# Four of eight K-pairs by seven products, and feature-major products sorted by length

## The chip, the cores and the metric

The kernel runs on one core of one Trainium2 chip. The metric is the device time of one execution in microseconds. Three runs of the kernel before took 2154.32, 2154.62 and 2155.61 us, median 2154.62. TensorE is called PE here, VectorE DVE, ScalarE ACT, GpSimd POOL, SyncE SP.

## The reference

A decoder trunk of two pre-norm layers on 256 tokens of width 2048, all in float32. The first layer's mixer is latent attention beside an mLSTM memory, the second's is a dilated attention. Each is followed by the MLP on which most of this change falls, with a hidden width of 8192:

```python
def rms_norm(x, g):
    y = x32 * lax.rsqrt(jnp.mean(x32 * x32, axis=-1, keepdims=True) + NORM_EPS)
    return (y * g.astype(jnp.float32)).astype(x.dtype)

def squared_relu_mlp(h, w1, w2):
    return jnp.square(jax.nn.relu(h @ w1)) @ w2

    for layer in range(DEPTH):                    # DEPTH = 2
        h = rms_norm(x, norm_mix[layer])
        ...                                       # mix: even or odd mixer of h
        x = x + mix
        x = x + squared_relu_mlp(rms_norm(x, norm_mlp[layer]), mlp_w1[layer], mlp_w2[layer])
    return rms_norm(x, norm_final)
```

## The kernel before

Every float32 operand of a large product is split into two parts: `hi`, the operand rounded to the matmul's reduced format by ACT (L129), and `lo`, the rest, by a DVE subtraction (L130). Of the four part products three are taken, all but lo x lo. Weights stream in 512 KB tiles `wr` through SP's queue into four buffers (L120); `wh` and `wl` have four each, so a tile's three forms live only for a few steps.

Two kinds of product are used. **Feature-major** (`steps_feats`, `mm_feats`, L152): the weight slice stands in the PE array and the activations move; `hi` meets both parts of them side by side (512 columns, L154) and `lo` meets their `hi` part (256 columns, L155). These are the MLP's up-projections (tile `h`), the odd layer's Q and K, and some of the even layer. **Token-major** (`mm_three`, L146): the activations stand and 512 weight columns move, three times.

The MLP runs in four quarters of 2048 hidden features. A quarter is eight chunks of up-projection (32 pairs of 512 and 256 columns each), whose results `h` are evacuated by `both` (ACT copy L269, DVE add L270), squared with ReLU on DVE (L1005, L1014) and split into `ht` or `pt`; then the down-projection, in two column halves of 1024 columns (`c` = 0 and 2). In a column half the 16 blocks of hidden features are taken as eight pairs. A pair is a 2x2 block product (two token blocks, two column blocks): plainly it takes eight products (`eight`: two steps of 12 matmuls), or, by sums of blocks made beforehand, seven (`seven`: 21 matmuls). For a seven DVE makes the weight sums `ta` (L206) and `tb` in two adds (L208, L209), and ACT and DVE split two raw tiles and the two sums. PE's results are gathered in eight PSUM banks: `ym` holds four products that enter several results, `yc(b, j)` those of one. `early_y` (L1026) adds the `ym` into the residual `x` after the last seven, `late_y` (L1045) the `yc` at the end of the half; both are on DVE. `SEVEN = 3` (L22) pairs go by seven.

The tile framework's scheduler sets each engine's order; every engine then runs its queue strictly in that order. In the last quarter of the first MLP only the first column half is done so; the other columns are plain matmuls (L1084, L1087) with the next norm's transposes (`turn`, L333) between them, and `n2.turn(3)` (L1099) follows.

Of the kernel before, what the change touches and what calls it, by code (L numbers as in the profile page):

```python
# [14 lines left out]
P = 128  # L15
S = 256
# [2 lines left out]
KD = D // P  # L19
FF = 8192  # L20
NQ = 4
SEVEN = 3  # L22
EPS = 1e-6
BIG = -3.0e38
MLA_SCALE = 192 ** -0.5
# [44 lines left out]
def trunk(ctx: ExitStack, tc: tile.TileContext, plan, a, c_first, c_even, c_odd, out):  # L70
# [78 lines left out]
        nc.tensor.matmul(ac, xh, lo, start=False, stop=False)  # L149
        nc.tensor.matmul(ac, xl, hi, start=False, stop=last)  # L150

    def mm_feats(ac, T, hi, lo, first, last):  # L152

        nc.tensor.matmul(ac, hi, T.rearrange("p a t -> p (a t)"), start=first, stop=False)  # L154
        nc.tensor.matmul(ac[:, :S], lo, T[:, 0, :], start=False, stop=last)  # L155

    def steps_tokens(Ts, w, c0, n, evac, kt=2, order=None, name="a", split_first=False):

# [20 lines left out]
    def steps_seven(pool, H, pairs, w, c, early, late, name="y"):  # L179

        box = {}
        rest = [k for k in range(len(H) // 2) if k not in pairs]  # L190

        def seven(k):
            def go():
                first, last = k == pairs[0], k == pairs[-1]
                if first:
                    box["m"] = {i: mis(f"{name}m{i}") for i in (1, 5, 7, 6)}
                    box["c"] = {i: acc(f"{name}c{i}") for i in ((0, 1), (1, 0), (0, 0), (1, 1))}
                m, cc = box["m"], box["c"]
                pt = H[2 * k][0]
                r0 = load(w, [(2 * k, c, 512), (2 * k + 1, c + 512, 512)], (2, 512))  # L200
                r1 = load(w, [(2 * k, c + 512, 512), (2 * k + 1, c, 512)], (2, 512))
                n_w[0] += 1
                ta = pool.tile([P, 2, 512], F32, name=f"ta{n_w[0]}", tag="ta", bufs=2)
                tb = pool.tile([P, 2, 512], F32, name=f"tb{n_w[0]}", tag="tb", bufs=1)
                h0, l0 = halves(r0)
                nc.vector.tensor_tensor(ta, r0, r1[:, 0:1, :].to_broadcast([P, 2, 512]), OP.add)  # L206
                h1, l1 = halves(ta, pool, "t", 3)
                nc.vector.tensor_tensor(tb[:, 0, :], ta[:, 0, :], r0[:, 1, :], OP.add)  # L208
                nc.vector.tensor_tensor(tb[:, 1, :], tb[:, 0, :], r1[:, 1, :], OP.add)  # L209
                h2, l2 = halves(tb, pool, "t", 3)  # L210
                h3, l3 = halves(r1[:, 1:2, :])

                def product(ac, i, h, l, j, last):
                    mm_three(ac, (pt[:, 0, i, :], pt[:, 1, i, :]), (h[:, j, :], l[:, j, :]), first, last)

                end = last and not rest
                product(m[1], 1, h0, l0, 0, last)
                product(m[5], 5, h1, l1, 0, last)
                product(m[7], 4, h1, l1, 1, last)
                product(m[6], 6, h2, l2, 0, last)  # L220
                product(cc[1, 0], 3, h2, l2, 1, end)
                product(cc[0, 1], 7, h0, l0, 1, end)
                product(cc[0, 0], 0, h3, l3, 0, end)
                if last:
                    early(m[1], m[5], m[6], m[7])
            return go

        def eight(k, j):
            def go():
                cc = box["c"]  # L230
                hi, lo = weights(w, 2 * k, 2, c + 512 * j, 512)
                for i in range(2):
                    for b in range(NB):
                        mm_three(cc[b, j], operand(H[2 * k + i], b), (hi[:, i, :], lo[:, i, :]),
                                 (b, j) == (1, 1) and k == rest[0] and i == 0, k == rest[-1] and i == 1)
                if k == rest[-1] and j == 1:
                    late(cc)
            return go

        out = []  # L240
        for i, k in enumerate(pairs):
            out += [seven(k)] + [eight(r, j) for r in rest[i:i + 1] for j in range(2)]
        return out + [eight(r, j) for r in rest[len(pairs):] for j in range(2)]

    def steps_feats(Ts, w, c0, evac, n=256, name="f"):

        box = {}
        groups = [range(i, i + 4) for i in range(0, len(Ts), 4)]

        def make(gi, g):  # L250
            def go():
                if gi == 0:
                    box["a"] = [acc(f"{name}{f}") for f in range(n // P)]
                hi, lo = weights(w, g[0], 4, c0, n)
                for j, k in enumerate(g):
                    for f in range(n // P):
                        mm_feats(box["a"][f], Ts[k], hi[:, j, f * P:(f + 1) * P], lo[:, j, f * P:(f + 1) * P],
                                 k == 0, k == len(Ts) - 1)
                if gi == len(groups) - 1:
                    for f in range(n // P):  # L260
                        evac(f, box["a"][f])
            return go

        return [make(gi, g) for gi, g in enumerate(groups)]
# [30 lines left out]
    first = const.tile([P, 2 * P], F32, name="first")  # L295
    ident, cum = first[:, :P], first[:, P:]
    gates_b = cols[:, 112:120]
    even_c = const.tile([P, 1536], F32, name="even_c", tag="tab")

    def col(name, i):  # L300
        j = _COLUMN[name] + i
# [137 lines left out]
    def even_layer(norm):  # L439
# [2 lines left out]
        mpool[0] = st.enter_context(tc.tile_pool(name="ev_mix", bufs=1))  # L442
        big = st.enter_context(tc.tile_pool(name="ev_big", bufs=1))
        sm = st.enter_context(tc.tile_pool(name="ev_small", bufs=1))
        causal, causal_t = even_c[:, 0:384], even_c[:, 384:768]
        c64 = even_c[:, 768:896].rearrange("p (b d) -> p b d", b=NB)
        s64 = even_c[:, 896:1024].rearrange("p (b d) -> p b d", b=NB)
# [354 lines left out]
    def odd_layer(norm):  # L802
# [1 line left out]
        st = ExitStack()  # L804
        mpool[0] = st.enter_context(tc.tile_pool(name="od_mix", bufs=1))
        sm = st.enter_context(tc.tile_pool(name="od_small", bufs=1))
        odd_c = const.tile([P, 1536], F32, name="odd_c", tag="tab")
        nc.gpsimd.dma_start(odd_c[:, :896], c_odd)
        dil = odd_c[:, 0:384]
        X = norm.T  # L810
        norm.close()
        rstd = norm.rstd()
        N = {}
# [62 lines left out]
                    + steps_tokens(X, w_qkv, 4096 + 512 * g, 512, evac_v(g), name="v"))  # L876

        g0 = group(0)
        run(g0[:1], [tables], g0[1:])
        for g in range(1, 4):  # L880
            weave(group(g), side(g - 1))

# [106 lines left out]
    def mlp(layer, norm, nxt):  # L989
# [6 lines left out]
        def evac_h(H):  # L996
            def make(c):
                box = {}

                def go(f, ac):  # L1000
                    u = sm.tile([P, S], F32, name="hu", tag="hu", bufs=2)
                    both(sm, u, ac, "h")
                    if c >= SEVEN:
                        r = sm.tile([P, S], F32, name="hr", tag="hr", bufs=2)
                        nc.vector.scalar_tensor_tensor(r, u, 0.0, u, OP.max, OP.mult)  # L1005
                        H[2 * c + f] = sm.tile([P, 2, S], FR, name="ht", tag="ht", bufs=2 * (NF // 2 - SEVEN) + 1)
                        split_to(H[2 * c + f], r)
                        return
                    if f == 0:
                        box["r"] = sm.tile([P, 8, P], F32, name="hp", tag="hp", bufs=2)  # L1010
                    r = box["r"]
                    dst = r[:, 1:3, :] if f == 0 else r[:, 0:4:3, :]
                    v = u.rearrange("p (b t) -> p b t", b=NB)
                    nc.vector.scalar_tensor_tensor(dst, v, 0.0, v, OP.max, OP.mult)  # L1014
                    if f == 1:
                        nc.vector.tensor_tensor(r[:, 4:6, :], r[:, 1:3, :], r[:, 2:4, :], OP.subtract)
                        nc.vector.tensor_tensor(r[:, 6, :], r[:, 5, :], r[:, 1, :], OP.subtract)
                        nc.vector.tensor_tensor(r[:, 7, :], r[:, 0, :], r[:, 6, :], OP.add)
                        pt = sm.tile([P, 2, 8, P], FR, name="pt", tag="pt", bufs=SEVEN)
                        nc.scalar.activation(pt[:, 0], r, AF.Copy)  # L1020
                        nc.vector.tensor_tensor(pt[:, 1], r, pt[:, 0].bitcast(F32), OP.subtract)
                        H[2 * c], H[2 * c + 1] = (pt, 0), (pt, 1)
# [35 lines left out]
        for q in range(NQ):  # L1058
            H = [None] * NF
            ev = evac_h(H)  # L1060
            for c in range(NF // 2):
# [7 lines left out]
                else:  # L1069
                    run(steps)  # L1070
            wq = ("mlp_w2", layer, q * (FF // NQ))
            for c in (0, 2):
                if c == 2 and q == NQ - 1:
                    break
                steps = steps_seven(sm, H, list(range(SEVEN)), wq, c * 512, early_y(c), late_y(c))
                run(steps)
            if q < NQ - 1:
                continue
            if nxt is None:
                finish(H, wq, evac_y, scale, sm)  # L1080
                continue
            nxt.stats(0)
            nxt.stats(1)
            weave(steps_tokens(Late(H), wq, 1024, 512, evac_y(2), name="y"),  # L1084
                  [lambda: nxt.turn(0), lambda: nxt.turn(1)])
            nxt.stats(2)
            weave(steps_tokens(Late(H), wq, 1536, 512, evac_y(3), name="y"), [lambda: nxt.turn(2)])  # L1087
        if nxt is not None:
            nxt.stats(3)
        return st  # L1090

# [4 lines left out]
    st.close()  # L1096
    n2 = Norm("norm_mix", 16, "mix1")
    mlp(0, n1, n2).close()
    n2.turn(3)  # L1099
    n3 = Norm("norm_mlp", 16, "mlp1")  # L1100
    mix, w_out, ev, side, st = odd_layer(n2)
    project(mix, w_out, ev, side, n3)
# [52 lines left out]
```

## Time and profile before

| | |
|---|---|
| median of 3 runs | 2154.62 us |
| profiled execution, its own time | 2153.76 us |
| its span, first to last instruction | 2151.8 us |
| busy: PE, DVE, ACT | 2132.0 (99%), 1578.6 (73%), 1108.8 (52%) us |
| matmuls | 11088 |
| mean granted clock of PE | 0.999 |
| PE's share of the chain that ended last | 88%, DVE 6% |
| DMA | 404.51 MB, mean 188 GB/s |

A matmul's printed duration is modelled and reaches into the next one, so a busy PE is not PE at its peak: the price of one is the step between starts, read from the timeline. In a timeline the columns are start, duration, engine, line, operation, output<-inputs, shapes, count; in square brackets the idle time before the row and what ended it. Rows that follow each other in one line of code are merged.

### The profile page before, as it was taken

To read this page: it belongs to the slowest core of one execution; us is meant where nothing else is said; L and a number is where in the kernel's file an instruction comes from. 1 tells how busy PE (TensorE), PEld (TensorE's weight loads), DVE (VectorE), ACT (ScalarE), POOL (GpSimd) and SP (SyncE) were. 2 spreads that over 40 slices of the span, in tenths; PEclk is the share of its full clock that TensorE was granted. 3 is DMA by queue.
4 is the path that set the end of the run, shared out by engine and by line. 5 is a ranking of instruction groups with operands and counts; after the bars stand their busy time and mean duration, and the time that the engine had idled before them with its cause. 6 is when DMAs were issued, how large, how long until landed. Compare 5 with 4: busy or idle time off the path is not lost.

```text
span 2151.8 us, 29351 instructions
## 1 busy us (share of the span) xinstructions
PE 2132.0 (99%) x11088; PEld 1827.6 (85%) x11088; DVE 1578.6 (73%) x2279; ACT 1108.8 (52%) x1550; POOL 5.6 (0%) x12
## 2 busy tenths in 40 slices
PE   9999999999999999999999999999999999999998
PEld 8998888888888888888888888888878888888887
DVE  5668556788788779778667667557887797797685
ACT  6576445554554455445544444555544554554453
POOL 0000000000000000000000000000000000000000
PEclk9999999999999999999999999999999999999999
DMA  8555555656555555656565545555565556556664
GB/s 290 166 166 172 166 183 171 195 194 205 186 193 196 189 185 198 196 179 210 168 198 168 178 162 186 165 181 186 192 201 190 186 198 194 179 194 206 207 198 143
DMA packets 115278, 404.51 MB, mean 188 GB/s; under 512 B 12928, under 2 KB 13568, under 8 KB 115136
## 3 DMA queue, kind: packets, MB, share of 16 engines
q1 hardware_dynamic: 114624, 401.07, 57.3%
q8 instruction: 87, 1.43, 0.3%
q0 software_dynamic: 368, 1.51, 0.2%
q14 instruction: 55, 0.45, 0.1%
q10 hardware_dynamic: 144, 0.06, 0.0%
HBM read 400.49 MB, written 2.10 MB: 187 GB/s over the span
## 4 chain that ended last, share of the span: by engine, by line
PE 88%; DVE 6%; DMA 2%; issue 2%; ACT 1%; SPq 0%; DVEq 0%; POOLq 0%; POOL 0%; ACTq 0%
PE h L154 22%; PE h L155 11%; DVE wl L130 3%; PE q L154 3%; PE k L154 3%; PE o L148 3%; PE o L150 3%; PE o L149 3%; DMA wr<-in_mlp_w 2%; PE v L148 2%; PE v L150 2%; PE v L149 2%; PE k L155 1%; PE q L155 1%; PE qk L154 1%
## 5 line engine op out<-in xcount | busy, mean ns | idle before, releaser
L130 DVE TENSOR_TENSOR wl<-wr,wh 128x1024 fp32r<-128x1024 f32 (+4 forms) x769 | 893.8, 1170 | 388.2 <-ACT wh L129 383.7
L129 ACT ACTIVATE wh<-wr 128x1024 fp32r<-128x1024 f32 (+4 forms) x769 | 777.9, 1014 | 735.7 <-issue 173.6
L154 PE MATMUL h<-T,wh 128*128 128x512 f32 x2048 | 721.0, 398 | 0.0
L155 PE MATMUL h<-T,wl 128*128 128x256 f32 x2048 | 572.7, 280 | 0.0
L154 PEld LDWEIGHTS h<-T,wh 128*128 128x128 f32 x2048 | 384.6, 188 | 94.0 <-DVE T L288 0.3
L155 PEld LDWEIGHTS h<-T,wl 128*128 128x128 f32 x2048 | 386.3, 189 | 0.4
L148 PE MATMUL o<-wh,M 128*128 128x512 f32 x256 | 102.3, 400 | 0.0
L150 PE MATMUL o<-wh,M 128*128 128x512 f32 x256 | 99.8, 390 | 0.0
L149 PE MATMUL o<-wl,M 128*128 128x512 f32 x256 | 99.6, 389 | 0.0
L269 ACT ACTIVATE bt_h<-h 128x256 f32<-128x256 f32 x128 | 48.7, 381 | 87.6 <-PE h L155 87.5
L154 PE MATMUL q<-T,wh 128*128 128x512 f32 x256 | 92.3, 403 | 0.0
L154 PE MATMUL k<-T,wh 128*128 128x512 f32 x256 | 92.2, 403 | 0.0
L270 DVE TENSOR_TENSOR hu<-h,bt_h 128x256 f32<-128x256 f32 x128 | 53.2, 421 | 33.0 <-ACT bt_h L269 33.0
L148 PE MATMUL v<-wh,T 128*128 128x512 f32 x192 | 77.4, 403 | 0.0
L150 PE MATMUL v<-wh,T 128*128 128x512 f32 x192 | 75.0, 390 | 0.0
L149 PE MATMUL v<-wl,T 128*128 128x512 f32 x192 | 74.8, 390 | 0.0
L206 DVE TENSOR_TENSOR ta<-wr,wr 128x1024 f32<-128x1024 f32 x42 | 51.4, 1225 | 31.4 <-DMA wr<-in_mlp_w 30.9
L149 PE MATMUL ym<-wl,pt 128*128 128x512 f32 x168 | 66.1, 393 | 5.9 <-DVE wl L130 5.9
L155 PE MATMUL k<-T,wl 128*128 128x256 f32 x256 | 71.9, 281 | 0.0
L155 PE MATMUL q<-T,wl 128*128 128x256 f32 x256 | 71.8, 281 | 0.0
L148 PE MATMUL ym<-wh,pt 128*128 128x512 f32 x168 | 65.9, 392 | 0.2 <-ACT wh L129 0.2
L150 PE MATMUL ym<-wh,pt 128*128 128x512 f32 x168 | 65.4, 389 | 0.0
(944 smaller groups left out, 3749.1 us busy)
## 6 DMA issues: line engine op xcount, KB each, us to landing
wr<-in_mlp_w SPq DMA_DIRECT2D x512, 512.0 KB, 4.1
wr<-in_od_w_qkv SPq DMA_DIRECT2D x96, 512.0 KB, 3.6
wr<-in_ev_w_in SPq DMA_DIRECT2D x32, 512.0 KB, 3.6
wr<-in_ev_w_out SPq DMA_DIRECT2D x32, 512.0 KB, 3.5
wr<-in_od_w_out SPq DMA_DIRECT2D x32, 512.0 KB, 3.5
wr<-in_ev_w_in SPq DMA_DIRECT2D x24, 344.0 KB, 3.0
wr<-in_ev_w_in SPq DMA_DIRECT2D x15, 364.0 KB, 6.0
wr<-in_mla_w_ukv SPq DMA_DIRECT2D x8, 512.0 KB, 3.5
```

Source lines behind the costliest of these rows:

```text
L129: nc.scalar.activation(hi, raw, AF.Copy)
L130: nc.vector.tensor_tensor(lo, raw, hi.bitcast(F32), OP.subtract)
L148: nc.tensor.matmul(ac, xh, hi, start=first, stop=False)
L149: nc.tensor.matmul(ac, xh, lo, start=False, stop=False)
L150: nc.tensor.matmul(ac, xl, hi, start=False, stop=last)
L154: nc.tensor.matmul(ac, hi, T.rearrange("p a t -> p (a t)"), start=first, stop=False)
L155: nc.tensor.matmul(ac[:, :S], lo, T[:, 0, :], start=False, stop=last)
L206: nc.vector.tensor_tensor(ta, r0, r1[:, 0:1, :].to_broadcast([P, 2, 512]), OP.add)
L269: nc.scalar.activation(t, ac[:, S:], AF.Copy)
L270: nc.vector.tensor_add(out, ac[:, :S], t)
```

## The change

`SEVEN` becomes 4, and the eights stand so that the last two sevens of a column half follow each other: seven, eight, seven, eight, seven, seven, eight, eight. The second column half of the first MLP's last quarter goes by sevens too. Feature-major products of a group come as all 512-column ones, then all 256-column ones. ReLU and square are two ACT operations in place of one on DVE. The last two turns of the first MLP's next norm move behind the first two steps of the odd layer, and the tables of constants move to the layers' own memory.

```diff
-SEVEN = 3
+SEVEN = 4
-    def mm_feats(ac, T, hi, lo, first, last):
-        nc.tensor.matmul(ac, hi, T.rearrange("p a t -> p (a t)"), start=first, stop=False)
-        nc.tensor.matmul(ac[:, :S], lo, T[:, 0, :], start=False, stop=last)
+    def mm_feats(acs, Ts, hi, lo, first, last):
+        n, F = len(Ts), len(acs)
+        for j in range(n):
+            for f in range(F):
+                nc.tensor.matmul(acs[f], hi[:, j, f * P:(f + 1) * P], Ts[j].rearrange("p a t -> p (a t)"),
+                                 start=first and j == 0, stop=False)
+        for f in range(F):
+            for j in range(n):
+                nc.tensor.matmul(acs[f][:, :S], lo[:, j, f * P:(f + 1) * P], Ts[j][:, 0, :],
+                                 start=False, stop=last and j == n - 1)
...
-        out = []
+        out, rest_of = [], iter(rest)
         for i, k in enumerate(pairs):
-            out += [seven(k)] + [eight(r, j) for r in rest[i:i + 1] for j in range(2)]
-        return out + [eight(r, j) for r in rest[len(pairs):] for j in range(2)]
+            out.append([seven(k)])
+            if i != len(pairs) - 2:
+                out += [[eight(r, j) for j in range(2)] for r in [next(rest_of)]]
+        out += [[eight(r, j) for j in range(2)] for r in rest_of]
+        return sum(out, [])
...
-        odd_c = const.tile([P, 1536], F32, name="odd_c", tag="tab")
-        nc.gpsimd.dma_start(odd_c[:, :896], c_odd)
+        odd_c = sm.tile([P, 896], F32, name="odd_c")
+        nc.gpsimd.dma_start(odd_c, c_odd)
...
-        run(g0[:1], [tables], g0[1:])
+        run(g0[:2], [lambda: norm.turn(2), lambda: norm.turn(3)], g0[2:3], [tables], g0[3:])
...
                     both(sm, u, ac, "h")
+                    nc.scalar.activation(u, u, AF.Relu)
-                        nc.vector.scalar_tensor_tensor(r, u, 0.0, u, OP.max, OP.mult)
+                        nc.scalar.activation(r, u, AF.Square)
...
-                    nc.vector.scalar_tensor_tensor(dst, v, 0.0, v, OP.max, OP.mult)
+                    nc.scalar.activation(dst, v, AF.Square)
...
+            last = q == NQ - 1
             for c in (0, 2):
-                if c == 2 and q == NQ - 1:
+                if last and nxt is None and c == 2:
+                    finish(H, wq, evac_y, scale, sm)
                     break
                 steps = steps_seven(sm, H, list(range(SEVEN)), wq, c * 512, early_y(c), late_y(c))
+                if last and c == 2:
+                    nxt.stats(0)
+                    nxt.stats(1)
+                    steps = steps[:-1] + [lambda: nxt.turn(0)] + steps[-1:] + [lambda: nxt.turn(1)]
                 run(steps)
```

What this makes of the engines' queues, at three places. The first is PE in the first group of the first up-projection; `h_3547` and `h_3548` are its two accumulators, `T` the activations. Before:

```order
L154 MATMUL h_3547<-T_3252,wh_3551 128x512
L155 MATMUL h_3547<-T_3252,wl_3552 128x256
L154 MATMUL h_3548<-T_3252,wh_3551 128x512
L155 MATMUL h_3548<-T_3252,wl_3552 128x256
L154 MATMUL h_3547<-T_3255,wh_3551 128x512
L155 MATMUL h_3547<-T_3255,wl_3552 128x256
L154 MATMUL h_3548<-T_3255,wh_3551 128x512
L155 MATMUL h_3548<-T_3255,wl_3552 128x256
```

Now:

```order
L158 MATMUL h_3547<-T_3252,wh_3551 128x512
L158 MATMUL h_3548<-T_3252,wh_3551 128x512
L158 MATMUL h_3547<-T_3255,wh_3551 128x512
L158 MATMUL h_3548<-T_3255,wh_3551 128x512
L158 MATMUL h_3547<-T_3263,wh_3551 128x512
L158 MATMUL h_3548<-T_3263,wh_3551 128x512
L158 MATMUL h_3547<-T_3266,wh_3551 128x512
L158 MATMUL h_3548<-T_3266,wh_3551 128x512
L162 MATMUL h_3547<-T_3252,wl_3552 128x256
L162 MATMUL h_3547<-T_3255,wl_3552 128x256
L162 MATMUL h_3547<-T_3263,wl_3552 128x256
L162 MATMUL h_3547<-T_3266,wl_3552 128x256
```

Lengths alternated row by row; now eight of 512 stand together and eight of 256 behind them.

The second place is DVE at the end of the first column half of the first MLP's first quarter, where the second half begins; `x_73`, `x_77`, `x_74` and `x_78` with L1049 (now L1058) are the late adds of the half that ends, `ta`, `tb` and `wl` belong to the half that begins. Before:

```order
L130 TENSOR_TENSOR wl_4796<-ta_4788,wh_4795 128x1024
L209 TENSOR_TENSOR tb_4789<-tb_4789,wr_4786 128x512
L1049 SCALAR_TENSOR_TENSOR x_73<-yc(0, 0)_4441,iv_mlp_3679,x_73 128x512
L1049 SCALAR_TENSOR_TENSOR x_77<-yc(1, 0)_4440,iv_mlp_3679,x_77 128x512
L130 TENSOR_TENSOR wl_4802<-tb_4789,wh_4801 128x1024
L1049 SCALAR_TENSOR_TENSOR x_74<-yc(0, 1)_4439,iv_mlp_3679,x_74 128x512
L1049 SCALAR_TENSOR_TENSOR x_78<-yc(1, 1)_4442,iv_mlp_3679,x_78 128x512
L130 TENSOR_TENSOR wl_4806<-wr_4786,wh_4805 128x512
L130 TENSOR_TENSOR wl_4833<-wr_4830,wh_4832 128x1024
L130 TENSOR_TENSOR wl_4851<-wr_4848,wh_4850 128x1024
```

Now:

```order
L1058 SCALAR_TENSOR_TENSOR x_73<-yc(0, 0)_4456,iv_mlp_3681,x_73 128x512
L1058 SCALAR_TENSOR_TENSOR x_77<-yc(1, 0)_4455,iv_mlp_3681,x_77 128x512
L214 TENSOR_TENSOR ta_4813<-wr_4809,wr_4811 128x1024
L130 TENSOR_TENSOR wl_4831<-wr_4811,wh_4830 128x512
L1058 SCALAR_TENSOR_TENSOR x_74<-yc(0, 1)_4454,iv_mlp_3681,x_74 128x512
L1058 SCALAR_TENSOR_TENSOR x_78<-yc(1, 1)_4457,iv_mlp_3681,x_78 128x512
L130 TENSOR_TENSOR wl_4821<-ta_4813,wh_4820 128x1024
L216 TENSOR_TENSOR tb_4814<-ta_4813,wr_4809 128x512
L130 TENSOR_TENSOR wl_4858<-wr_4855,wh_4857 128x1024
L217 TENSOR_TENSOR tb_4814<-tb_4814,wr_4811 128x512
L130 TENSOR_TENSOR wl_4876<-wr_4873,wh_4875 128x1024
L130 TENSOR_TENSOR wl_4827<-tb_4814,wh_4826 128x1024
```

The split of `ta` and the second sum `tb` stood ahead of the four late adds, and the split of `tb` among them. Now the split of `ta`, both sums `tb` and, behind two splits of the eight that follows, the split of `tb` stand behind all four. This order is the same in all seven down-projections that have a second half by sevens.

The third place is PE just there, in the second half's first seven, from the fifth product on; `wl_4821` is the split of `ta`, `wh_4826` and `wl_4827` those of `tb`. Now:

```order
L149 MATMUL ym_4802<-wl_4821,pt 128x512
L150 MATMUL ym_4802<-wh_4820,pt 128x512
L149 MATMUL ym_4803<-wl_4821,pt 128x512
L150 MATMUL ym_4803<-wh_4820,pt 128x512
L148 MATMUL ym_4804<-wh_4826,pt 128x512
L148 MATMUL yc(1, 0)_4806<-wh_4826,pt 128x512
L148 MATMUL yc(0, 1)_4805<-wh_4815,pt 128x512
L149 MATMUL yc(0, 1)_4805<-wl_4816,pt 128x512
L150 MATMUL yc(0, 1)_4805<-wh_4815,pt 128x512
L148 MATMUL yc(0, 0)_4807<-wh_4830,pt 128x512
L149 MATMUL ym_4804<-wl_4827,pt 128x512
```

Ahead of these stand the three products of `ym_4801` and the two with `wh_4820`, the rounding of `ta`. So nine products come before the first that needs `tb`, as before, where they stood three by three, each with its two parts of the weights.

## Rows read from the trace of the kernel before

**Rows 1.** Stages: us; busy us (count) of PE, PEld, DVE, ACT, POOL; clock; DMA share, GB/s.
```profile
529.70:620.10 90.40, 90.40 (x513) 78.44 (x512) 63.21 (x87) 44.69 (x60) 0.00 (x0) 1.00 0.57 183
620.10:704.50 84.40, 83.35 (x368) 68.56 (x367) 75.56 (x87) 43.07 (x48) 0.00 (x0) 1.00 0.61 203
```

**Rows 2.** PE's timeline: start us, duration us, operation; 512-column and 256-column runs, first and last.
```profile
678.02 0.39 PE L148 MATMUL yc(0, 0)_6325<-wh,ht 128*128 128x512 f32 x1
...
683.46 0.39 PE L148 MATMUL ym<-wh,pt 128*128 128x512 f32 x1
...
2132.04 0.28 PE L148 MATMUL z<-wh,pt 128*128 128x256 f32 x1
...
2143.44 0.28 PE L150 MATMUL z<-wh,ht 128*128 128x256 f32 x1
```

**Rows 3.** PE's timeline: alternating pairs, first quarter (379.13 on) and third quarter (704.54 on).
```profile
379.13 0.39 PE L154 MATMUL h<-T,wh 128*128 128x512 f32 x1
...
445.69 0.39 PE L148 MATMUL ym<-wh,pt 128*128 128x512 f32 x1
...
704.54 0.39 PE L154 MATMUL h<-T,wh 128*128 128x512 f32 x1
704.77 0.28 PE L155 MATMUL h<-T,wl 128*128 128x256 f32 x1
...
794.98 0.40 PE L148 MATMUL ym<-wh,pt 128*128 128x512 f32 x1
```

**Rows 4.** DVE's timeline, first column half: steps between starts of operations without idle time.
```profile
635.02 0.69 DVE L209 TENSOR_TENSOR tb<-tb,wr 128x512 f32<-128x512 f32 x1
635.63 1.22 DVE L130 TENSOR_TENSOR wl<-ta,wh 128x1024 fp32r<-128x1024 f32 x1
636.77 1.22 DVE L130 TENSOR_TENSOR wl<-wr,wh 128x1024 fp32r<-128x1024 f32 x1
...
645.73 0.75 DVE L1030 SCALAR_TENSOR_TENSOR x<-yq,iv_mlp,x 128x512 f32<-128x512 f32 x1
646.39 0.75 DVE L1030 SCALAR_TENSOR_TENSOR x<-yp,iv_mlp,x 128x512 f32<-128x512 f32 x1
```

**Rows 5.** ACT's groups by line: evacuation copies; count, busy us, mean ns, idle before.
```profile
L269 ACT ACTIVATE bt_h<-h 128x256 f32<-128x256 f32 x128 | 48.7, 381 | 87.6 <-PE h L155 87.5
```

**Rows 6.** DVE's timeline at the start of the second column half.
```profile
659.36 0.68 DVE L209 TENSOR_TENSOR tb<-tb,wr 128x512 f32<-128x512 f32 x1
...
661.28 1.21 DVE L130 TENSOR_TENSOR wl<-tb,wh 128x1024 fp32r<-128x1024 f32 x1
...
663.08 0.74 DVE L1049 SCALAR_TENSOR_TENSOR x<-yc(1, 1)_5985,iv_mlp,x 128x512 f32<-128x512 f32 x1
663.73 2.95 DVE L130 TENSOR_TENSOR wl<-wr,wh 128x512 fp32r<-128x512 f32 x3
668.00 1.23 DVE L206 TENSOR_TENSOR ta<-wr,wr 128x1024 f32<-128x1024 f32 x1 [1.31 <-DMA wr<-in_mlp_w]
```

**Rows 7.** PE's timeline there: the half's first product, and the later wait.
```profile
661.61 0.39 PE L148 MATMUL ym<-wh,pt 128*128 128x512 f32 x1
...
675.63 0.51 PE L149 MATMUL ym<-wl,pt 128*128 128x512 f32 x1 [1.05 <-DVE wl L130]
```

**Rows 8.** PE's and ACT's timelines: a rounding, and an operand's release to ACT.
```profile
677.11 0.39 PE L150 MATMUL yc(0, 1)_6323<-wh,pt 128*128 128x512 f32 x1
...
669.26 1.06 ACT L129 ACTIVATE wh<-ta 128x1024 fp32r<-128x1024 f32 x1 [0.62 <-DVE ta L206]
...
677.59 1.06 ACT L129 ACTIVATE wh<-wr 128x1024 fp32r<-128x1024 f32 x1 [2.85 <-PE yc(0, 1)_6323 L150]
```

**Rows 9.** PE's groups by line, 4.2 to 12 us and 16 to 60 us.
```profile
L149 PE MATMUL c<-wl,T 128*128 128x364 f32 x7 | 3.7, 530 | 0.0
...
L149 PE MATMUL c<-wl,T 128*128 128x364 f32 x50 | 16.4, 329 | 0.0
```

More of the change, by code (lines that the diff above doesn't have):

```diff
@@ L254, in go @@
                 hi, lo = weights(w, g[0], 4, c0, n)
[L255 to L258, printed above, removed]
+                mm_feats(box["a"], [Ts[k] for k in g], hi, lo, gi == 0, gi == len(groups) - 1)
                 if gi == len(groups) - 1:
@@ L297, in trunk @@
     gates_b = cols[:, 112:120]
-    even_c = const.tile([P, 1536], F32, name="even_c", tag="tab")
     def col(name, i):
@@ L444, in even_layer @@
         sm = st.enter_context(tc.tile_pool(name="ev_small", bufs=1))
+        even_c = sm.tile([P, 1536], F32, name="even_c")
         causal, causal_t = even_c[:, 0:384], even_c[:, 384:768]
@@ L806, in odd_layer @@
         sm = st.enter_context(tc.tile_pool(name="od_small", bufs=1))
-        odd_c = const.tile([P, 1536], F32, name="odd_c", tag="tab")
-        nc.gpsimd.dma_start(odd_c[:, :896], c_odd)
+        odd_c = sm.tile([P, 896], F32, name="odd_c")
+        nc.gpsimd.dma_start(odd_c, c_odd)
         dil = odd_c[:, 0:384]
-        X = norm.T
+        X = Late(norm.T)
         norm.close()
@@ L1071, in mlp @@
             wq = ("mlp_w2", layer, q * (FF // NQ))
+            last = q == NQ - 1
             for c in (0, 2):
-                if c == 2 and q == NQ - 1:
+                if last and nxt is None and c == 2:
+                    finish(H, wq, evac_y, scale, sm)
                     break
                 steps = steps_seven(sm, H, list(range(SEVEN)), wq, c * 512, early_y(c), late_y(c))
+                if last and c == 2:
+                    nxt.stats(0)
+                    nxt.stats(1)
+                    steps = steps[:-1] + [lambda: nxt.turn(0)] + steps[-1:] + [lambda: nxt.turn(1)]
                 run(steps)
[L1077 to L1085, printed above, removed]
+        if nxt is not None:
             nxt.stats(2)
-            weave(steps_tokens(Late(H), wq, 1536, 512, evac_y(3), name="y"), [lambda: nxt.turn(2)])
-        if nxt is not None:
             nxt.stats(3)
@@ L1098, in trunk @@
     mlp(0, n1, n2).close()
-    n2.turn(3)
     n3 = Norm("norm_mlp", 16, "mlp1")
```

## The prediction

> **What bounds the kernel now.** I read the busy time by stage first. In the second quarter of the first MLP, TensorE (PE) is busy for all 90.40 us of the up-projection and for 83.35 of the 84.40 us of the down-projection; VectorE (DVE) has 63.21 and 75.56 us of work in them, ScalarE (ACT) 44.69 and 43.07 [rows 1]. So PE bounds both stages, and DVE is close behind in the down-projection alone: that is where the change adds DVE work.
>
> Then the timeline of PE, where a matmul's price is the step from one start to the next, since its printed duration overlaps the next one. Twenty-four 512-column products run from 678.02 to 683.46, 0.2267 us each; 95 steps of 256 columns from 2132.04 to 2143.44, 0.120 each [rows 2]. Up-projection products alternate 512 and 256: 256 such pairs from 704.54 to 794.98, 0.3533 a pair; but in the first quarter, 192 pairs from 379.13 to 445.69, 0.3467 [rows 3]. Two runs of equal length would cost 0.2267 + 0.120 = 0.3467. So alternation costs 6.6 ns a pair in the later quarters and nothing in the first; why they differ, the rows don't say.
>
> Last the DVE queue. Steps: 0.61 us for a 128x512 subtract or add, 1.14 for 128x1024, 0.66 for a 512-wide scaled add [rows 4]. A seven-product step costs DVE 4 x 1.14 + 3 x 0.61 = 6.4 us against 21 x 0.2267 = 4.76 on PE; an eight-product pair 2 x 1.14 = 2.3 against 5.44. DVE loses on each seven and recovers on each eight, and it runs its queue strictly in the order shown above.
>
> **The change, part by part.**
>
> Fewer products. A column half goes from 3 sevens and 5 eights (183 matmuls) to 4 and 4 (180). There are 14 halves before; after there are 15, the last quarter of the first MLP turning its 192 plain matmuls into one more half. 14 x 183 + 192 - 15 x 180 = 54 matmuls less: 54 x 0.2267 = **-12.2 us**, if PE stays the bound.
>
> Sorted products. A group of 16 becomes eight of 512 and eight of 256, with two changes of length left instead of sixteen. At 0.3467 plus some 0.6 ns for these, 0.347 a pair. Up-projections other than the quick chunks of the two first quarters have 1,664 pairs, the other feature-major products some 500 that I put at the same 0.353: 2,160 x 6.0 ns = **-13.0 us**. Bounds: 0, if the excess belongs to the 256-column matmuls and not to the change; -18, if all 2,768 pairs gain 6.6. I take -13 because both steps of the sum are measured in runs.
>
> Here the Trainium skill speaks otherwise ("TensorE: Matmul & The Clock Gate", section "Back-to-back issue gap"): columns / 2.4 GHz plus 2.5 ns, 0.216 and 0.109 us. By that rule a sorted pair is an estimated 0.325, and sorting would give some -61 us. The rows above, 0.2267 and 0.120 in long equal runs, do not agree with it.
>
> ReLU and square on ACT. 128 DVE operations of 128x256 go, 256 ACT operations come. Nearest row, ACT on 128x256: 381 ns [rows 5], 98 us over eight up-projections in which ACT is idle for some 45 of 90 us each [rows 1]. Cost and gain 0: DVE is 27 us short of full there, and the activations are first read a stage later. If the cover were gone, it would be at most 12 us a stage; I give that no chance, since only half is used.
>
> The hand-over between column halves. This is the term that decides. In the new DVE order the last split operand of the second half's first seven is behind the first half's last accumulation. Before, its sum `tb` was complete at 659.36 + 0.61 and its split began at 661.28, with PE starting the half at 661.61 [rows 6, 7]; only `x_74`, `x_78` and later splits came behind. Now the queue runs x_78 (0.66), split of `ta` (1.14), `tb` (0.61), a split (1.14), `tb` (0.69 to its end), and then ACT must round `tb` (1.06) [rows 8] before PE's tenth product can start. With T1 the start of the half on PE without a wait: x_78 needs the last product before T1, which ends 0.39 after its start at T1 - 0.23, and a reader follows PE's end by 0.09 (677.11 + 0.39 against 677.59) [rows 8]. So x_78 cannot start before T1 + 0.25; the sum is T1 + 0.25 + 0.66 + 1.14 + 0.61 + 1.14 + 0.69 + 0.05 + 1.06 + 0.05 = T1 + 5.65. PE has nine products, 2.04 us, to run meanwhile. **3.6 us of wait is the least** that this order allows. DVE adds to it, as it arrives late. Counting from the start of the first half, DVE cannot split the second eight's last operand until PE has left that buffer, after 45 products and their end at 10.4; ACT (1.06) and DVE (1.14) are through with it at 12.7. From there to x_78 stand two sevens (6.4 and, with its waits for its own results, 6.6), four splits (4.6), eight early combinations (5.35), one split, one `ta`, one half split and three late adds (4.9), and one rounding on ACT that nothing covers (1.2): 12.7 + 29.05 = 41.7, against T1 = 180 x 0.2267 = 40.8. So x_78 starts at T1 + 0.9 and PE waits 2.04 to 6.3: **4.3 us**, in two pieces.
>
> The second half afterwards. The next seven's raw tiles are freed by `tb`'s second sum at T1 + 5.1 and refilled 3.6 us later (663.73 + 0.61 to 668.00 in the trace) [rows 6]; DVE resumes there. Laid against PE in the same way, the second seven is in time by 0.4 us, and the fourth, directly behind the third and with an eight's split ahead of its own last one, is late by **0.6** (0 to 1.5). In the first half the same place is in time by 0.4.
>
> So 4.9 us a down-projection, in seven of them (the eighth has no second seven half): 34.3 us. Today each of six has a wait of 1.2 (675.63, 1.05 of it idle), all on the same operand, the first one 0.8 [rows 7]: 7.0 that go. Net **+27.3 us** (+18 at the floor of 3.6; +42 at 7.0).
>
> The moved turns and tables. The sixteen transposes are on PE's queue before and after; what changes is that the first Q products wait for tiles that DVE makes one by one, with splits of 1.14 in between: +0.5 (0 to 2). The odd constants are now loaded when the MLP's memory falls free, not long before; some ten us of DVE work stand ahead of their first reader, against 3.6 for the nearest load, so 0.
>
> Sum: -12.2 - 13.0 + 27.3 + 0.5 = +2.6 us. The profiled execution took 2153.76 us (span 2151.8, 2.0 around it), the median of the runs is 0.9 above it: 2153.76 + 2.6 + 0.9, rounded, **2157 us**.
>
> **Rivals.**
>
> *The floor decides* (chance 0.20). DVE reaches x_78 in time, the fourth seven is covered, and each hand-over costs 3.6. For it: DVE is idle for 8.8 us of today's stage. Against it: the 32 operations counted above, in a row and without a gap. Sum -6.7: 2148.
>
> *DVE becomes the bound of the stage* (0.18; slower). Two sevens in a row cost DVE 13.0 us against 9.5 on PE. If it enters the third seven less than about 3.3 us ahead, PE waits at the fourth in both halves, and the backlog lengthens the hand-over too. My margin in the first half is 0.4 us; with 1 us lost there and 1 more behind, 7 us a stage: +17, 2172.
>
> *Sorting gives nothing* (0.10). For it: the first quarters run alternating pairs at 0.3467 without it [rows 3], so alternation as such need not cost. Against it: both long runs are flat. +13: 2170.
>
> *The clock falls at the hand-over* (0.04). PE pauses for some 1.5 and 2.5 us within 5, seven times; today's longest idle is about 1, and the granted clock stays at full speed, 2.4 GHz [rows 1]. At the program's start the first 364-column products took 0.53 us, later ones 0.33 [rows 9]; 21 such products a hand-over, at 0.2 us each, make 29 us: 2186. The Trainium skill warns of just this (same page, section "A second HAM failure mode: psum-queue depth-cycling": frequent small pauses between matmul groups make the clock go back and forth). In the trace the six pauses of before did not, so by that rule the trace does not agree so far.
>
> By the rule on the issue gap above, the sum would be -45, 2109 us; I give it 0.02.
>
> **How the numbers follow.** The forecast has 0.46, with its own range 2150 to 2164 (hand-over 3.9 to 5.5, sorting -10 to -15). About 0.2% (4.3 us) can be told from no change: faster is below 2150.3, slower above 2158.9. The floor gives 0.15 of faster, the forecast's lower end and the issue-gap case the rest: 0.21. Slower: DVE-bound, no sorting gain and the clock 0.31, and the forecast's upper part 0.07: 0.38. Same: 0.41. The range 2145 to 2173 leaves out the clock, the issue gap and the tails of two others.
>
> **What would show it.** PE's steps in sorted runs at 0.227 and 0.120, and up-projections of later quarters at about 89 us. In each of seven down-projections, two pauses shortly after the second half's start, the longer one of about 2.5 us ended by ACT's rounding of `tb`, with x_78, the split of `ta` and two others on DVE before it; stages of 86.5 us instead of 84.4. The prediction is wrong if these pauses are missing or sum to less than 3.6, if sevens three and four show waits of over 1.5, or if the sorted runs are not quicker.

## The result and the profile after

The changed kernel took 2174.66 us (median of 4 runs, 2172.40 to 2176.72) against 2154.62 (4 runs): ratio 1.0092, 95% interval [1.0074, 1.0109]. It is slower by 20 us, past the end of the range (2173), where 2157 was forecast. Its profiled execution took 2174.26 us, its span 2172.5.

Stages of the first MLP, with the columns of [rows 1]: the first quarter's down-projection, the second quarter's up-projection, and in three pieces the second quarter's down-projection, cut at its hand-over:

```profile
445.40:533.70 88.30, 84.64 (x363) 68.37 (x362) 80.95 (x93) 46.30 (x56) 0.00 (x0) 0.98 0.56 185
533.70:623.00 89.30, 89.30 (x513) 78.60 (x512) 60.06 (x76) 54.58 (x87) 0.00 (x0) 1.00 0.59 195
623.00:664.76 41.76, 41.66 (x184) 34.14 (x183) 38.44 (x46) 23.55 (x32) 0.00 (x0) 1.00 0.56 177
664.76:674.80 10.04, 6.59 (x20) 4.47 (x19) 8.72 (x10) 3.27 (x4) 0.00 (x0) 0.83 0.56 197
674.80:711.00 36.20, 36.20 (x160) 29.65 (x160) 33.57 (x39) 19.54 (x21) 0.00 (x0) 1.00 0.61 192
```

The up-projection fell from 90.40 to 89.30 us, and the second quarter's down-projection, 84.40 before, takes 88.00 (41.76 + 10.04 + 36.20). Nearly all of it is lost in ten microseconds: ahead of the hand-over and from 674.80 on PE is busy almost without a gap, between them for 6.59 of 10.04 us, and only there the clock is not full. PE's timeline in that stretch (columns of [rows 2], idle time and its releaser in brackets):

```profile
664.31 0.39 PE L148 MATMUL ym<-wh,pt 128*128 128x512 f32 x1
...
665.02 0.73 PE L148 MATMUL ym<-wh,pt 128*128 128x512 f32 x2
666.98 0.50 PE L149 MATMUL ym<-wl,pt 128*128 128x512 f32 x1 [1.22 <-DVE wl L130]
...
667.78 0.40 PE L150 MATMUL ym<-wh,pt 128*128 128x512 f32 x1
670.40 0.50 PE L148 MATMUL ym<-wh,pt 128*128 128x512 f32 x1 [2.23 <-ACT wh L129]
...
672.34 0.63 PE L149 MATMUL ym<-wl,pt 128*128 128x512 f32 x1
672.77 0.63 PE L150 MATMUL ym<-wh,pt 128*128 128x512 f32 x1
...
675.08 0.39 PE L149 MATMUL yc(0, 0)_6385<-wl,ht 128*128 128x512 f32 x1
```

Three things are to be seen. The two pauses are the predicted ones: 1.39 us more than a step ahead of the product that needs the split of `ta`, 2.40 ahead of the one that needs the rounding of `tb`. Behind the second the steps are 0.43 us (672.34 to 672.77) instead of 0.2267: PE runs at 1.2 GHz. And at 675.08 it runs at 2.4 GHz again. The same three stand in all seven hand-overs, with pauses of 1.24 to 1.40 and 2.39 to 2.40 us and one stretch of low clock each, 3.4 us long, in the first MLP's last quarter 6.8:

```profile
1026.35:1033.17 6.82, 6.12 (x14) 4.79 (x15) 3.82 (x4) 2.30 (x4) 0.00 (x0) 0.50 0.78 273
493.87:497.28 3.41, 3.41 (x9) 2.66 (x9) 1.82 (x3) 1.06 (x1) 0.00 (x0) 0.50 0.98 354
671.37:674.77 3.40, 3.40 (x10) 2.64 (x9) 2.08 (x3) 1.06 (x1) 0.00 (x0) 0.50 0.93 355
```

DVE's queue in front of the long pause, in the place of [rows 6] (the first row is the late add `x_78`), and ACT's rounding of `tb` that ends the pause:

```profile
665.05 0.73 DVE L1058 SCALAR_TENSOR_TENSOR x<-yc(1, 1)_6035,iv_mlp,x 128x512 f32<-128x512 f32 x1
665.71 1.21 DVE L130 TENSOR_TENSOR wl<-ta,wh 128x1024 fp32r<-128x1024 f32 x1
666.84 0.68 DVE L216 TENSOR_TENSOR tb<-ta,wr 128x512 f32<-128x512 f32 x1
667.45 1.21 DVE L130 TENSOR_TENSOR wl<-wr,wh 128x1024 fp32r<-128x1024 f32 x1
668.58 0.68 DVE L217 TENSOR_TENSOR tb<-tb,wr 128x512 f32<-128x512 f32 x1
```

```profile
669.29 1.06 ACT L129 ACTIVATE wh<-tb 128x1024 fp32r<-128x1024 f32 x1 [3.38 <-DVE tb L217]
```

With T1 = 664.31, `x_78` starts at T1 + 0.74 and PE's tenth product at T1 + 6.09; the prediction had 0.9 and 6.3.

The sorted products: a group is eight 512-column products, eight 256-column ones, and the next group.

```profile
556.00 2.00 PE L158 MATMUL h<-T,wh 128*128 128x512 f32 x8
557.84 1.12 PE L162 MATMUL h<-T,wl 128*128 128x256 f32 x8
558.79 2.00 PE L158 MATMUL h<-T,wh 128*128 128x512 f32 x8
```

558.79 - 556.00 is 2.79 us for eight pairs, 0.349 a pair, where [rows 3] have 0.3533 in the later quarters and 0.3467 in the first one. A later up-projection gains 1.08 us; each of the two first ones loses some 0.7.

### The profile page after: what moved, and what is told of

The parts are those of the page before. It is cut to its first block, busy times and chain, and to the rows that moved or that the text cites. A ratio compares the mean times of both kernels' runs of the same rounds, so it can differ in the third digit from the quotient of the medians.

```text
span 2172.5 us, 29631 instructions
## 1 busy us (share of the span) xinstructions
PE 2131.6 (98%) x11034; PEld 1826.3 (84%) x11034; DVE 1607.7 (74%) x2265; ACT 1216.2 (56%) x1833; POOL 5.6 (0%) x12
## 4 chain that ended last, share of the span: by engine, by line
PE 78%; DVE 14%; DMA 4%; issue 3%; ACT 1%; SPq 0%; DVEq 0%; POOLq 0%; POOL 0%; ACTq 0%
PE h L158 19%; PE h L162 10%; DVE wl L130 7%; DMA wr<-in_mlp_w 4%; PE q L158 3%; PE k L158 3%; PE o L150 3%; PE o L148 3%; PE o L149 3%; PE v L148 2%; PE v L150 2%; PE v L149 2%; DVE ta L214 2%; PE k L162 1%; PE q L162 1%
## 5 line engine op out<-in xcount | busy, mean ns | idle before, releaser
L158 PE MATMUL h<-T,wh 128*128 128x512 f32 x2048 | 513.4, 392 | 0.0
L162 PEld LDWEIGHTS h<-T,wl 128*128 128x128 f32 x2048 | 279.4, 190 | 20.0
L162 PE MATMUL h<-T,wl 128*128 128x256 f32 x2048 | 285.6, 282 | 0.0
L148 PE MATMUL ym<-wh,pt 128*128 128x512 f32 x240 | 95.2, 401 | 16.0 <-ACT wh L129 15.9
L129 ACT ACTIVATE wh<-ta 128x1024 fp32r<-128x1024 f32 x60 | 63.6, 1061 | 77.3 <-DVE ta L214 77.2
L129 ACT ACTIVATE wh<-tb 128x1024 fp32r<-128x1024 f32 x60 | 63.2, 1053 | 66.6 <-DVE tb L217 66.6
L150 PE MATMUL ym<-wh,pt 128*128 128x512 f32 x240 | 94.8, 395 | 0.0
L130 DVE TENSOR_TENSOR wl<-tb,wh 128x1024 fp32r<-128x1024 f32 x60 | 73.3, 1221 | 22.9 <-ACT wh L129 22.9
L1011 ACT ACTIVATE hu<-hu 128x256 f32<-128x256 f32 x128 | 50.5, 408 | 51.3 <-DVE hu L278 51.3
L130 DVE TENSOR_TENSOR wl<-ta,wh 128x1024 fp32r<-128x1024 f32 x60 | 73.1, 1219 | 2.7 <-ACT wh L129 2.7
L148 PEld LDWEIGHTS ym<-wh,pt 128*128 128x128 f32 x240 | 44.9, 189 | 30.0 <-ACT wh L129 21.7
```

Source lines behind the costliest of these rows:

```text
L129: nc.scalar.activation(hi, raw, AF.Copy)
L130: nc.vector.tensor_tensor(lo, raw, hi.bitcast(F32), OP.subtract)
L148: nc.tensor.matmul(ac, xh, hi, start=first, stop=False)
L158: nc.tensor.matmul(acs[f], hi[:, j, f * P:(f + 1) * P], Ts[j].rearrange("p a t -> p (a t)"), start=first and j == 0, stop=False)
L162: nc.tensor.matmul(acs[f][:, :S], lo[:, j, f * P:(f + 1) * P], Ts[j][:, 0, :], start=False, stop=last and j == n - 1)
L1011: nc.scalar.activation(u, u, AF.Relu)
```

## The experiments

My theory after the traces: the fourth seven, through DVE's order and lateness at the hand-over, costs the pauses and the clock; sorting is worth half of what I said. The rivals: the squares on ACT; DVE too full in any half with four sevens; a clock that falls for other reasons than the pauses. Each run is given with its time, its ratio to the kernel before and the 95% interval of that, and PE's mean granted clock where it matters.

**Three sevens.** `SEVEN = 3` in the changed kernel, in the old order.

> The changed kernel with three sevens a column half, in the old order (seven, eight, seven, eight, seven, three eights), so 3 x 15 = 45 products more than the changed kernel; sorting, squares on ACT and the moved turns stay. Theory 1 (the fourth seven makes DVE late at the hand-over, PE pauses for 3.8 us there and then runs at the lower clock for 3.4 us): both go, down-projections are back at 84.4 us, and what is left against before is the sorting as the two traces show it (six later up-projections 1.08 us shorter, two first ones 0.67 longer) and 9 products: 2154.6 - 5.1 - 2.0 = 2147.5 us, granted clock 0.999. Theory 2 (the loss comes from the squares on ACT or from another order of DVE's queue, whatever the number of sevens): it stays above 2165 us.

2148.26 us, 0.9976 [0.9966, 0.9985], clock 0.999. So the fourth seven, with the order of steps that comes with it, makes the changed kernel 26.4 us slower, though it takes 45 products away. (Four sevens with an eight behind each were not run.) The idle time of PE before `ym`, by what ended it (us, times), first in the changed kernel, then here:

```profile
  ACT wh L129: 15.9, 8
  DVE wl L130: 10.7, 12
```

```profile
  DVE wl L130: 6.6, 7
  ACT wh L129: 0.6, 2
```

**Sorting alone.** The new `mm_feats` in the kernel before.

> The kernel before with the sorted feature-major products and nothing else. Theory 1 (sorting is worth what the two traces show in the up-projections, 6 x 1.08 - 2 x 0.67 = 5.1 us, and little elsewhere): 2149.5 us; later up-projections 89.4 us, first ones 90.5. Theory 2 (the prediction's 6.0 ns a pair, hidden in the changed kernel by something else): 2141.6 us. Theory 3 (it gives nothing by itself): 2154.6 us.

2147.86 us, 0.9970 [0.9958, 0.9983]: 6.3 us, theory 1 (5.1) and not 13.0. The up-projections are 89.36 and 90.56 us, so the first quarters lose here too.

**The pauses filled.** In the second half's first seven:

```
+ if first and c == 1024:
+     for _ in range(6):
+         nc.tensor.matmul(m[5], pt[:, 0, 1, :], h0[:, 0, :], start=True, stop=True)
  product(m[5], 5, h1, l1, 0, last)
...
+     for _ in range(10):
+         nc.tensor.matmul(m[6], ...)
  product(m[6], 6, h2, l2, 0, last)
```

> The changed kernel with 16 products more at each of the seven hand-overs: 6 ahead of the second product of the second half's first seven, 10 ahead of the fourth, into banks that the real products then start anew, from operands that are there already; 16 x 0.2267 = 3.63 us in place of 3.8 us of pause. Theory 1 (it is the pauses that lower the clock): the granted clock stays at full speed in all seven, PE's end of the hand-over comes at the same time, and the 1.6 us lost behind each (3.3 in the one that stays low twice as long) come back: 2174.7 - 12.9 = 2161.8 us. Theory 2 (the clock falls for another reason, such as the number of products): 2174.7 us or more. Theory 3 (the pauses only move behind the added products, as DVE and ACT need the time that PE leaves them): clock low again, above 2175 us.

2169.46 us, 1.0070 [1.0058, 1.0083]; clock 0.999. The pauses are what lowers the clock, as theory 1 has it, but only 5 of the 12.9 us come back. The hand-over itself runs through; its own tenth product comes at T1 + 6.15 (T1 = 664.55), with the pauses at T1 + 6.09:

```profile
668.32 2.23 PE L233 MATMUL ym<-wh,pt 128*128 128x512 f32 x9
670.70 0.50 PE L148 MATMUL ym<-wh,pt 128*128 128x512 f32 x1
...
682.70 0.50 PE L149 MATMUL ym<-wl,pt 128*128 128x512 f32 x1 [1.22 <-DVE wl L130]
```

Then PE, quick again, stops at 682.70, in the next seven, for 1.42 us more than a step: DVE had stood still for its raw tiles.

```profile
675.07 1.23 DVE L214 TENSOR_TENSOR ta<-wr,wr 128x1024 f32<-128x1024 f32 x1 [3.16 <-DMA wr<-in_mlp_w]
```

Such stops, of 0.35 to 1.42 us, stand in all seven places now, and each is as long as the start of `ta` lies behind some T1 + 9.1 (here `ta` starts at T1 + 10.5). In the changed kernel `ta` starts at T1 + 8.5 to T1 + 10.3, in three of the seven places behind T1 + 9.1, and PE stops in none. One of the three, with T1 = 842.18:

```profile
852.03 1.23 DVE L214 TENSOR_TENSOR ta<-wr,wr 128x1024 f32<-128x1024 f32 x1 [2.51 <-DMA wr<-in_mlp_w]
```

There the slow clock hid a wait that comes into the open when the clock is kept. By these three starts it hid some 3.2 of the 12.9 us (an estimate). The filled run's time says nearly 8, but its tiles also landed later: in the place of 675.07 the changed kernel has `ta` at T1 + 8.6, which needs no stop at any clock. So the net price of the low clock is some 0.7 us a hand-over by the run and 1.4 by the estimate, not 1.8; why the tiles landed later is not shown.

**One pause filled.** Only the six, then only the ten products.

> The changed kernel with only the six products ahead of the second product of the second half's first seven, so that the pause of 1.4 us is filled and the one of 2.4 us stays. Theory 1 (the long pause alone lowers the clock): low clock behind each of seven hand-overs as in the changed kernel, 2174.7 us within 2. Theory 2 (it takes two pauses close together): full clock throughout, about 2169 us.

2174.85 us (2 runs), 1.0095 [1.0076, 1.0113]. The long pause is still 2.40 us in all seven places, and the clock fell at five of them; the first and the seventh stayed at full speed. The first place (its pause ends at 495.23) and the second (671.99):

```profile
489.00:497.60 8.60, 6.34 (x27) 4.60 (x26) 7.44 (x9) 3.66 (x4) 0.00 (x0) 1.00 0.42 142
497.60:501.00 3.40, 3.40 (x16) 2.81 (x16) 2.29 (x3) 1.86 (x3) 0.00 (x0) 1.00 0.72 261
...
671.80:675.00 3.20, 3.01 (x7) 2.43 (x8) 1.40 (x2) 0.56 (x2) 0.00 (x0) 0.50 0.93 279
```

So the long pause alone can do it, but need not: theory 1, with an exception that I can't explain.

> The changed kernel with only the ten products ahead of the fourth product, so that the pause of 2.4 us is filled and the one of 1.4 us stays. Theory 1 (the long pause lowers the clock): full clock throughout, about 2169 us. Theory 2 (any idle of 1.4 us does): low clock behind each hand-over, 2174.7 us within 2.

2169.01 us (2 runs), 1.0068 [1.0049, 1.0086], full clock. The edit did not do what its name says: seven of the ten went into the first pause, three into the second, and one pause of 1.6 us was left (1.4 in one of the seven places):

```profile
670.57 0.50 PE L148 MATMUL ym<-wh,pt 128*128 128x512 f32 x1 [1.43 <-ACT wh L129]
```

In all seven places a single pause of 1.4 to 1.6 us left the clock alone, so theory 2 (any idle of 1.4 us lowers it) is out; the first pause by itself, in its own place, was not run.

**The weights first.** The second half's first seven split into `prep` (loads, sums, splits) and products, the first moved ahead of the last eight:

```
+ first_half = first_half[:-2] + [prep] + first_half[-2:]
+ run(first_half, steps)
```

> The changed kernel with the weights of the second half's first seven loaded, added and split ahead of the first half's last eight, so that DVE's queue has all of that in front of the four late accumulations. Theory 1 (the order in which DVE's queue stands is the whole cause): no pause at the hand-over, no low clock, 7 x (3.8 + 1.6) + 1.7 = 39.5 us less: 2135 us. Theory 2 (DVE arrives late with all its work, the order only says which operand PE waits for): the splits now stand ahead of the last eight's own last operand, and PE waits there; two thirds of the pause stay, the clock falls or not: 2155 to 2175 us.

2153.74 us, 0.9998 [0.9989, 1.0007], clock 0.999. That is just under theory 2's range: nearly half of the pause went, and the clock held. The move takes 20.9 of the 26.4 us back. It is not a change of DVE's order alone: the scheduler also put ten of PE's `ym` products of the new half among the last eight's `yc` products. What is left of the pauses, with a `yc` product of the old half in front and one behind:

```profile
658.69 0.40 PE L148 MATMUL yc(1, 1)_6060<-wh,ht 128*128 128x512 f32 x1
659.30 0.73 PE L148 MATMUL ym<-wh,pt 128*128 128x512 f32 x2 [0.21 <-ACT wh L129]
660.88 0.50 PE L149 MATMUL ym<-wl,pt 128*128 128x512 f32 x1 [0.86 <-DVE wl L130]
...
662.58 0.50 PE L148 MATMUL ym<-wh,pt 128*128 128x512 f32 x1 [0.50 <-ACT wh L129]
662.91 0.39 PE L149 MATMUL yc(0, 0)_6059<-wl,ht 128*128 128x512 f32 x1
```

**The same with less DVE work.** `c` is 0 in the first column half.

```
- add(1, 0, q) ... add(0, 1, p); add(1, 1, q)
+ if c: add(1, 0, q) ... add(0, 1, p); add(1, 1, q)
```

> Weights_first, with three of the four early accumulations of the first column half left out (the output lacks them): 3 x 0.66 = 2.0 us of DVE work less just ahead of the hand-over, with the queue otherwise in nearly the same order. Theory 1 (what weights_first still waits at the hand-over, 0.38 + 1.03 + 0.67 us, is DVE arriving late): these go, up to 2.0 us in each of seven: 2153.7 - 14 = 2140 us. Theory 2 (it is ACT's roundings, the refill of the raw tiles or the order once more): less than a third of it goes, 2149 us or more.

2141.17 us, 0.9933 [0.9920, 0.9947]: 12.6 us less than with the weights first, 1.8 of the 2.0 us per hand-over that DVE was spared. The down-projection of the second quarter fell from 85.98 to 84.14 us, though it has the same 180 products a half. So what a better order leaves is DVE arriving late, and a microsecond taken off DVE there is nearly one of PE.

**Squares on DVE.** The run under this label was three_sevens a second time: 2149.45 us, 0.9977 [0.9967, 0.9987], which only says how well a run repeats.

> Three_sevens with the squared ReLU on DVE as in the kernel before (one DVE operation in place of ReLU and square on ACT). Theory 1 (the prediction's term of 0: ACT and DVE both have room in the up-projections, and TensorE sets their length): 2148.3 us within 2, up-projections as in three_sevens (90.6 and 89.36 us). Theory 2 (ACT's 256 operations more delay the roundings of the weights for the first sevens): it gains 3 us or more, by shorter down-projections.

The edit that was meant:

```
- nc.scalar.activation(u, u, AF.Relu)
...
- nc.scalar.activation(dst, v, AF.Square)
+ nc.vector.scalar_tensor_tensor(dst, v, 0.0, v, OP.max, OP.mult)
```

> Three_sevens with the squared ReLU on DVE as in the kernel before (one DVE operation in place of ReLU and square on ACT), which the run squares_on_dve was to test: that one ran three_sevens itself a second time. Theory 1 (the prediction's term of 0): within 2 us of three_sevens, up-projections as there (90.6 and 89.36 us). Theory 2 (ACT's 256 operations more delay the roundings of the weights for the first sevens): 3 us or more shorter, in the down-projections.

2148.28 us, 0.9971 [0.9961, 0.9982], against 2148.26 for three sevens: nothing, as the prediction had it.

**Three sevens, then four.**

```
- steps = steps_seven(sm, H, list(range(SEVEN)), ...)
+ steps = steps_seven(sm, H, list(range(SEVEN - (c == 0))), ...)
```

> The changed kernel with three sevens in the first column half of a down-projection (order: seven, eight, seven, eight, seven, three eights) and four in the second, so the hand-over between the halves is that of three sevens, and the half with four ends in front of an up-projection, in which DVE is idle for a third of the time. Theory 1 (a fourth seven costs only where DVE has to open another half directly behind it): 21 products less than with three and three, 2148.3 - 4.8 = 2143.5 us, no pause over 1.5 us at the hand-overs, granted clock 0.999. Theory 2 (four sevens make DVE late in any half, by the 0.6 us and more that the prediction gave to the fourth seven of the second half): seven halves lose at least 0.7 us each, 2148 us or more.

2144.00 us, 0.9953 [0.9941, 0.9966]. Theory 1: a fourth seven gains (4.3 of 4.8 us) where no other half opens behind it. Up- and down-projection of the second quarter:

```profile
531.73:621.09 89.36, 89.36 (x513) 78.65 (x512) 60.10 (x76) 54.61 (x87) 0.00 (x0) 1.00 0.58 194
621.09:704.82 83.73, 82.91 (x365) 67.99 (x364) 76.88 (x88) 44.93 (x54) 0.00 (x0) 1.00 0.58 195
```

**Fewer changes of length.** As the last, with every second group 256 columns first:

```
+ for go in (narrow, wide) if odd else (wide, narrow):
+     go()
```

> As three_then_four, and the sorted groups turned round in every second one (its eight 256-column products first, then its eight 512-column ones), so that a group boundary no longer changes the length: eight changes in each of 32 stretches become four. Theory 1 (what a sorted group costs over 8 x 0.2267 + 8 x 0.120 belongs to the changes of length: 233 ns at the last 256-column product of one group less 120, and 228 to 236 in the first 512-column ones, against 113 and 227): about half of 19 ns a group goes, 0.3 us an up-projection, later up-projections 89.05 us, some 2.5 us in all. Theory 2 (it belongs to the start of a new group, whose weights are another tile): up-projections stay at 89.36 us, time as in three_then_four.

2141.02 us, 0.9938 [0.9925, 0.9952]: 13 us less than before, the quickest of those that leave nothing out. Up-projections are at 89.06, as theory 1 has it:

```profile
529.44:618.50 89.06, 89.06 (x513) 78.71 (x512) 60.98 (x76) 53.29 (x87) 0.00 (x0) 1.00 0.57 194
```

```profile
533.16 3.82 PE L160 MATMUL h<-T,wh 128*128 128x512 f32 x16
536.82 2.08 PE L166 MATMUL h<-T,wl 128*128 128x256 f32 x16
538.73 3.82 PE L160 MATMUL h<-T,wh 128*128 128x512 f32 x16
```

Two groups take 538.73 - 533.16 = 5.57 us, where equal steps would make 5.547: one turn from 512 to 256 and back costs some 20 ns, whatever stands in the runs.

## Why the prediction was wrong

The profiled executions differ by 20.5 us; the sum had 2.6. Term by term, in us:

| term | predicted | measured | from |
|---|---|---|---|
| 54 products fewer | -12.2 | -12.2 | 0.2267 each; 21 of them gave 4.3 of 4.8 |
| sorting | -13.0 | -6.3 | sorting alone |
| hand-over, seven times | +30.1 | +28.4 | T1 + 6.09 against nine products' 2.04 |
| fourth seven | +4.2 | +4.7 | what remains |
| waits of before gone | -7.0 | -7.0 | none left at that place |
| clock | 0 | +12.9 | 6 x 1.6 + 3.3, by steps of 0.43 |
| squares on ACT | 0 | 0 | squares on DVE, second run |
| moved turns | +0.5 | 0 | below |

**The hand-over** was right in mechanism, place and size: two pauses, the longer 2.4 us, ended by ACT's rounding of `tb`, behind the four operations on DVE that were named. It was the term said to decide, and it is the largest. That DVE's queue is behind it is shown by two runs: the first seven's weights made earlier gave 20.9 us back (with some of PE's products moved too), and less DVE work another 12.6.

**The clock** is the step that failed: in the sum it stands at nothing. The prediction named this rival, with pauses of 1.5 and 2.5 us, and gave it 0.04 because the six pauses of about 1 us before had left the clock alone [rows 7]. That was reasoning from a pause half as long. The runs showed the clock at 1.2 GHz at all seven hand-overs. The rival's size was off too: some eight products a hand-over ran slowly, not 21, so 12.9 us and not 29, of which 5 (the filled run) to 10 (the estimate there) are its net price. The Trainium skill's rule that was weighed there ("TensorE: Matmul & The Clock Gate", section "A second HAM failure mode: psum-queue depth-cycling": small pauses between groups of matmuls can make the clock alternate) agrees with the changed kernel, seven times in seven, and did not show in the kernel before.

**Sorting** is the term that was mis-sized, by 6.7 us, in both of its steps. The 0.6 ns for "these" two changes of length is some 20 ns a group, 2.4 a pair. And the first quarters, which ran alternating pairs at 0.3467 [rows 3], were left out of the count, but sorting makes them slower, 0.349. The long runs it was read from [rows 2] had no change of length in them, so the price of a change was assumed.

**The fourth seven** has about the forecast size, in another place. It was put at 0.6 us in the second half and at nothing in the first, which was to be in time by 0.4. In the changed kernel the eight first halves take 41.08 to 42.45 us for 180 products, 40.80 by equal steps, and where they lose most PE waits for the split of `tb` of the fourth seven; the second halves lose 0.24 at theirs. Step by step that is 5.4 and 1.7 us where the other terms leave 4.7, so the table is exact to some 2 us. The longest such wait:

```profile
1007.40 0.50 PE L149 MATMUL ym<-wl,pt 128*128 128x512 f32 x1 [0.76 <-DVE wl L130]
```

**The moved turns.** Three sevens against sorting alone: the first MLP's last down-projection and the odd layer together are 0.6 us shorter, with 9 products (2.04 us) less. Of the 1.4 us between, 0.96 is the wait in the new second half (39.72 us for 171 products), so some 0.5 us is left for the turns; by the same count three-then-four leaves nothing, inside the 0 to 2 given.

**The rivals.** "The floor decides" was near for the pauses (3.8 us against 3.6), though `x_78` started 0.5 us behind the floor, and far off for the time. "DVE becomes the bound" gave 2172, close to the result by luck: its mechanism (waits at the fourth seven in both halves, 7 us a stage) is seen only in small, 0.3 to 1.6 us in the first halves. That DVE is late by about 2 us a hand-over is shown by weights_first_less_dve. With the clock kept by filled pauses the time was 2169.5; with the sorting as forecast the measured terms sum to 13.8, some 2168 us. Either alone would have stayed in the range.

What stays open: why two of seven equal pauses of 2.40 us left the clock up, why tiles landed later in the filled run, and why alternating pairs ran at 0.3467 in the first quarters of before.

## What to carry to other kernels

Taking products from a bound engine gains only where the engine that feeds it keeps up: look not at its share of the stage but at its queue where two of its heavy pieces meet, and put the extra work in the half that has slack behind it (with the same sorting, three and then four gained 10 us where four and four lost 20). Price a pause of TensorE at its length and, when it is longer than any that the trace of before has, give the clock a real chance. A low clock in front of an operand that is late anyway costs less than its slow steps add up to.

## What the runs showed of the hardware

- TensorE's granted clock was at 1.2 GHz for 3.4 us (once 6.8) behind pauses of 1.4 and 2.4 us; behind 2.4 alone in five cases of seven; behind 1.4 to 1.6 alone, behind 1.2 in the kernel before, and behind the idle times of 0.86 and 0.50 above, never.
- Alternating 512- and 256-column products have two steady patterns: in the later quarters of before, pairs of 0.361, 0.349 and 0.350 us in turn (mean 0.3533), in the first quarter pairs of 0.343 and 0.350 (0.3467). Each held to the end of its stage.
- A change between 512 and 256 columns and back costs some 20 ns beside equal steps of 0.2267 and 0.120.
